# Two inverse roots as a GpSimd power and a log sigmoid from the sigmoid, in a hybrid encoder block

## The chip, the cores and the metric

The kernel runs on one core of a Trainium2 chip. The metric is the device time of one execution in microseconds (us). Before the change the median of three runs is 942.79 us (942.76 to 943.74).

## The reference, cut to what matters

One layer on a sequence of 512 tokens with 1024 features, all in float32: a half-step feed-forward, a mixer of two branches, a second half-step feed-forward and a last norm. The two places that the change touches are in the mixer:

```python
def layer_norm(x, g, b):
    mu = jnp.mean(xf, axis=-1, keepdims=True)
    xc = xf - mu
    y = xc * lax.rsqrt(jnp.mean(xc * xc, axis=-1, keepdims=True) + EPS)
    return (y * g + b)
...
u = a * jax.nn.sigmoid(g)                       # branch A: 512 channels
y = depthwise_causal_conv(u, width=31) + conv_b
y_conv = jax.nn.silu(layer_norm(y, ln_g, ln_b))
...
log_f = jax.nn.log_sigmoid(f_logit)             # branch B: 8 heads of 64
cum = jnp.cumsum(log_f, axis=1)
s = q @ k.T * scale + cum[q] - cum[k]           # causal softmax, times v
...
y = concat([rms_norm(y_conv, out_norm_conv), rms_norm(y_attn, out_norm_attn)])
x = x + y @ w_out
```

The convolution branch thus has two norms in a row: the layer norm over its channels and, after the swish, the RMS norm of the branch output. Each needs 1/sqrt(mean square + 1e-6) for every token.

## The kernel before, in words

Features lie on the 128 partitions and the 512 tokens along the free dimension. TensorE multiplies in a reduced float32 form; each weight and each activation is held as a high and a low part, and a product is three matmuls per block of 128 (high by high, low by high, high by low). Every weight tile of 128x1024 is loaded on SyncE's queue, rounded by ScalarE into `whi` and subtracted by VectorE into `wlo` (`cast`, lines 507 to 510). This goes on through the whole kernel, three loads ahead and two splits ahead.

The program is written as a list of operations for a planner (class `Plan`, lines 172 to 388). `record` takes each operation and its dependences, `price` (lines 252 to 293) gives it a planned duration, and `schedule` (lines 295 to 382) simulates the engines and sets the order of the instructions on each of them: at each step the operation that can start earliest, ties broken by a rank that is the planned length of what hangs on it plus an urgency. ScalarE's functions that need an activation table name it, a change of table is planned at 1.3 us (`SWITCH`, line 175) and lowers the rank by 40 (`PENALTY`, line 81). On the chip each engine then runs its list strictly in order and waits only for semaphores. A changed price, operation or engine thus may change the order everywhere behind it. The loads of the activation tables themselves are not in the program; they are put in ahead of a function that the active table lacks.

The mixer's pieces are listed in `ORDER` (line 60): `c0 c1 c2 v c3 a0 a1 n a2 a3 w0 w1 w2 w3`. Here `c` is the projection, gate (a sigmoid on ScalarE) and convolution of one tile of 128 channels; the 31 taps of tiles 1 and 3 run on VectorE, those of tiles 0 and 2 as a scaled copy on ScalarE and an addition on GpSimd. `v` (`values`, lines 963 to 1020) is the projection of the values and the forget gates, `a` is the attention of two heads (lines 1047 to 1157), `n` the norms of the convolution branch (`conv_norm`, lines 1160 to 1180) and `w` the output projection.

The log sigmoid (lines 1003 to 1016) is computed on a 128x32 tile: ScalarE gives p = exp(-|z|), and VectorE then computes min(z, 0) - 2 artanh(p / (p + 2)) with a series, sixteen instructions joined into one block.

A norm's statistic goes through the class `Stats`: squares, a sum over the partitions by matmuls into a compact 128x128 tile of PSUM (`ssq_*`, 4 groups of 32 partitions for 4 groups of 128 tokens), then `rstd` (lines 594 to 607): ScalarE takes the root with scale 1/n and bias eps into `rc_*`, VectorE the reciprocal in place, `spread` lets TensorE copy the result to all partitions (`rb_*`), and ScalarE copies that to SBUF (`rstd_*`). `conv_norm` calls this twice, for `ln` and for `conv`. Its squares are GpSimd's (`sq_ln`, `sq_conv`), the subtraction of the mean and the multiplication by the scale VectorE's (`acc`), the swish and the high part `yh` ScalarE's, and the low part `yl` VectorE's. All other norms of the kernel call `rstd` in the same way.

In the traces nearly every instruction has line 248, where the planner emits it; instructions are told apart by their tiles.

Of the kernel before, what the change touches and what calls it, by code (L numbers as in the profile page):

```python
# [32 lines left out]
AF = mybir.ActivationFunctionType  # L33
ALU = mybir.AluOpType
AX = mybir.AxisListType

P = 128
# [134 lines left out]
class Plan:  # L172
# [79 lines left out]
    def price(self, op, engine, method, args, kwargs, out):  # L252

        n = out.n if isinstance(out, View) else 512
        if engine == "PE":
            if method != "matmul":
                return n * 0.00084, None
            part = args[1].at[0].size / P
            if args[1].buf.dt != F32:
                return 0.0133 + n / 2400.0, None  # L260
            if part > 0.5:
                return 2 * max(0.02 + n * 0.00069, 0.1), None
            op.tiled = part
            return (0.13 if part > 0.3 else 0.084) * max(n, 64) / P, None
        if method == "dma_start" and engine != "Q":
            return 0.1, None
        psum = any(isinstance(v, View) and v.buf.psum for v in list(args) + list(kwargs.values()))
        if engine == "S":
            cost = (0.143 if psum else 0.2) + n * 0.00083
            if method == "copy":  # L270
                return cost, None
            if isinstance(kwargs.get("scale"), View) or isinstance(kwargs.get("bias"), View):
                cost += 0.09
            if "accum_out" in kwargs:
                op.late = 0.1
            return cost, None if args[2] in (AF.Copy, AF.Square, AF.Identity) else args[2]
        if engine == "G":
            op.port = 1.0
            return 0.1 + n * (0.00233 if method.startswith("tensor_") else 0.0008), None
        if engine == "Q":  # L280
            op.bytes += n * 4 * P
            return 0.4, None
        if method == "tensor_tensor_scan":
            return 0.06 + n * 0.0022, None
        if method == "reciprocal":
            return 0.15 + n * 0.0062, None
        if method in ("tensor_copy", "tensor_scalar") and not psum:
            return 0.15 + n * 0.0006, None
        if not psum:
            op.port = 1.0  # L290
        if method == "scalar_tensor_tensor":
            return 0.15 + n * 0.00118, None
        return 0.15 + n * 0.00105, None
# [106 lines left out]
def block_kernel(ctx: ExitStack, tc, x_d, w13a, w2a, wag, wvf, wqk, wo, w13b, w2b, par_d, out_d):  # L400
    nc = tc.nc
    plan = Plan(tc)
    V, S, PE = plan.engine("V", nc.vector), plan.engine("S", nc.scalar), plan.engine("PE", nc.tensor)
    G, Q = plan.engine("G", nc.gpsimd), plan.engine("Q", nc.sync)
# [6 lines left out]
    def tile_(shape, tag, name, bufs=1, dt=F32):  # L411
        return plan.tile(sb, shape, dt, tag, name, bufs)

    def bank(tag, name, bufs=1):
        return plan.tile(pp, [P, T], F32, tag, name, bufs)

    def product_bank(name):
        return bank("mm", name, 3)
# [22 lines left out]
    eps = tile_([P, 1], "eps", "eps")  # L441
    G.memset(eps, EPS)
    scrap = tile_([P, 57], "scrap", "scrap")[:, :1]
    with plan.urgent(6000.0):
# [4 lines left out]
    ident16 = tile_([P, P], "ident16", "ident16", 1, BF16)  # L449
    G.affine_select(out=ident16, in_=ones, pattern=[[-1, P]], compare_op=ALU.is_equal, fill=0.0,  # L450
                    base=0, channel_multiplier=1)
    sel = tile_([P, NT, P], "sel", "sel")
    G.memset(sel, 0.0)
    mask16 = tile_([P, P], "mask16", "mask16", 1, BF16)
# [17 lines left out]
    for w13, w2 in ((w13a, w2a), (w13b, w2b)):  # L472
# [6 lines left out]
        if w13 is w13a:  # L479
            for piece in ORDER.split():  # L480
                n = int(piece[1:] or 0)
# [52 lines left out]
    class Stats:  # L534
# [56 lines left out]
            plan.join(None)  # L591
            return pb

        def rstd(self, keep=True):
            if self.acc is not None:
                self.sum([self.acc] + self.wait, True)
            w = self.w
            with plan.urgent(URGENT_STATS):
                c = self.compact = tile_([P, P], "rc", f"rc_{self.name}", 2)[:, :w]
                S.activation(c, self.ps[:, :w], AF.Sqrt, bias=eps, scale=1.0 / self.n)  # L600
                V.reciprocal(c, c)
                pb = self.spread(c)
                if not keep:
                    return pb
                r = tile_([P, T], "rstd", f"rstd_{self.name}", 2)
                S.copy(r, pb)
            return r
# [3 lines left out]
    def in_turn(step):  # L611

        for o in stream:
            step.before[id(o)] = o
# [282 lines left out]
    w = tile_([P, 2, KD, P], "vt", f"w{EARLY}", 1, F32R)  # L897
# [65 lines left out]
    def values():  # L963
        plan.urgency = URGENT_V
        pr = bank("misc", "pr", MISC)
        PE.transpose(pr[:, :P], st.compact, ident)
        rcol = tile_([P, NT], "rcol", "rcol")
        V.tensor_copy(rcol, pr[:, 0:P:32])
        plan.urgency = 0.0
        for c in range(2):  # L970
            pv = [product_bank(f"pv{c}_{t}") if t < 2 else bank("s", f"pv{c}_{t}", 2) for t in range(NT)]
            for kh in range(2):
                hi, lo = unit()
                for t in range(NT):
                    ts_ = slice(t * P, (t + 1) * P)
                    o = pv[t][:, :VC]
                    head = None
                    for k in range(KD // 2):
                        kk = kh * (KD // 2) + k
                        step = plan.join("PE", head)  # L980
                        if head is None:
                            head = step
                            in_turn(step)
                        PE.matmul(o, xh[kk][:, ts_], hi[:, k], start=kk == 0, stop=False)
                        PE.matmul(o, xh[kk][:, ts_], lo[:, k], start=False, stop=False)
                        PE.matmul(o, xl[kk][:, ts_], hi[:, k], start=False, stop=kk == KD - 1)
                        plan.join(None)
                    stream[:] = [step]
            plan.urgency = URGENT_V
            for t in range(NT):  # L990
                rc = rcol[:, t:t + 1]
                S.activation(vt[:, t, 4 * HD * c:4 * HD * (c + 1)], pv[t][:, :4 * HD], AF.Copy, scale=rc)
                V.scalar_tensor_tensor(zf[:, t, 4 * c:4 * c + 4], pv[t][:, 4 * HD:VC], rc,
                                       par[:, G_FB + 4 * c:G_FB + 4 * c + 4], ALU.mult, ALU.add)
            plan.urgency = 0.0

        plan.urgency = URGENT_LF
        lf, e1, e2, e3 = (tile_([P, NT, H], n, n) for n in ("lf", "e1", "e2", "e3"))  # L1000
        ps = plan.tile(pp, [P, 16, NT, H], F32, "pt", "e", PT)
        p1, p2, p3, p4 = (ps[:, n] for n in range(4))
        V.scalar_tensor_tensor(e1, zf, -1.0, zf, ALU.mult, ALU.min)
        S.activation(p1, e1, AF.Exp)
        plan.join("V")
        V.tensor_scalar(p2, p1, 2.0, None, ALU.add)
        V.reciprocal(e2, p2)
        V.tensor_mul(p3, p1, e2)
        V.tensor_mul(e1, p1, e2)
        V.tensor_mul(p4, p3, e1)  # L1010
        V.tensor_scalar(e3, p4, 1.0 / 17.0, None, ALU.mult)
        for n in (15, 13, 11, 9, 7, 5, 3):
            V.scalar_tensor_tensor(e3, e3, 1.0 / n, p4, ALU.add, ALU.mult)
        V.scalar_tensor_tensor(e3, e3, 1.0, p3, ALU.add, ALU.mult)
        V.tensor_scalar(p2, zf, 0.0, None, ALU.min)
        V.scalar_tensor_tensor(lf, e3, -2.0, p2, ALU.mult, ALU.add)
        plan.join(None)

        plan.urgency = 0.0
        return lf  # L1020
# [139 lines left out]
    def conv_norm():  # L1160
        ln = Stats("mean", DC)
        for i in range(NC):
            ln.pair(conv[i], i == NC - 1, mean)
        c = tile_([P, P], "rc", "rc_mean", 2)
        S.copy(c, ln.ps[:, :P])
        pm = ln.spread(c)
        ln = Stats("ln", DC)
        for i in range(NC):
            V.tensor_sub(conv[i], conv[i], pm)
            ln.pair(ln.square(conv[i], G), i == NC - 1)  # L1170
        lr = ln.rstd()
        stats = Stats("conv", DC)
        for i in range(NC):
            V.tensor_mul(conv[i], conv[i], lr)
            S.activation(conv[i], conv[i], AF.Silu, bias=par[:, G_LNB + i:G_LNB + i + 1],
                         scale=par[:, G_LNG + i:G_LNG + i + 1])
            stats.pair(stats.square(conv[i], G), i == NC - 1)
            yh[i], yl[i] = slot(2 * i, f"yh{i}", F32R), slot(2 * i + 1, f"yl{i}", F32R)
            split(yh[i], yl[i], conv[i], par[:, G_OC + i:G_OC + i + 1])
        return stats.rstd()  # L1180

    def w_out(part, d, w, r):

# [13 lines left out]
    for piece in ORDER.split():  # L1197
        n = int(piece[1:] or 0)
# [10 lines left out]
        else:  # L1209
# [3 lines left out]
            for j in range(2):  # L1213
                w = unit()
# [59 lines left out]
```

## Time and profile before

| | before |
|---|---|
| median of three runs | 942.79 us |
| the profiled execution's own time | 943.71 us |
| its span in the trace | 942.0 us |
| feed-forward 1 | 0 to about 362 us |
| mixer | about 362 to 577 us |
| feed-forward 2 and the last norm | about 577 to 942 us |
| activation table loads on ScalarE | 15, 1283 ns each |
| GpSimd additions and products of 128x512 | 1292 to 1516 ns by group, 1126 ns for `sq_ln` |

The profile's times are from the start of the span. "PE" is TensorE with its matmuls, "PEld" its weight loads, "DVE" VectorE, "ACT" ScalarE, "POOL" GpSimd and "SP" SyncE, whose queue carries the loads. A row of instructions in time has the start, the duration, the engine, the line, the operation, the output tile and the inputs, the shapes, how many were merged, and in brackets the idle time of the engine before it with what ended it. Matmuls are pipelined and their ends are modelled, so TensorE's busy time says that it had work, not that it ran at its peak.

### The profile page before, as it was taken

What the parts mean: (1) busy time and instruction counts of PE and PEld (TensorE: products, weight loads), DVE (VectorE), ACT (ScalarE), POOL (GpSimd) and SP (SyncE); (2) the same over time, 40 slices, a digit from 0 to 9 for tenths busy, and PEclk for the clock granted to TensorE, in tenths of its full rate; (3) what the DMA queues carried; (4) which work ended last, traced back from release to release, by engine and by line L of the source; (5) the groups of instructions that cost most, each with busy time, mean ns of one, the idle gap of its engine ahead of it and who ended that gap; (6) DMA issues with size and microseconds to landing.
All of it is one profiled execution on the core that took longest, in us unless ns stands there. A gap on an engine that the chain in (4) does not pass through costs nothing.

```text
span 942.0 us, 13470 instructions
## 1 busy us (share of the span) xinstructions
PE 930.2 (99%) x5277; PEld 794.3 (84%) x5277; DVE 655.2 (70%) x990; ACT 434.2 (46%) x678; POOL 154.7 (16%) x132
## 2 busy tenths in 40 slices
PE   9999999999999999999999999999999999999997
PEld 7888999988999888897776777888899988999887
DVE  6655877756876475799987776555777755876554
ACT  7433433334333245676878655333433333433344
POOL 1000211001112000889763000000111001111000
PEclk9999999999999999999999999999999999999999
DMA  7222323132333133323211222222332222323122
GB/s 253 85 92 93 131 90 112 69 107 73 134 112 107 51 97 104 91 93 110 91 68 47 66 67 90 90 90 95 125 117 90 90 90 90 124 100 98 65 84 90
DMA packets 34207, 91.19 MB, mean 97 GB/s; under 512 B 3544, under 2 KB 13912, under 8 KB 34144
## 3 DMA queue, kind: packets, MB, share of 16 engines
q1 hardware_dynamic: 33600, 90.13, 29.0%
q8 instruction: 41, 0.67, 0.3%
q10 hardware_dynamic: 544, 0.20, 0.1%
q14 instruction: 22, 0.18, 0.1%
HBM read 88.21 MB, written 2.11 MB: 96 GB/s over the span
## 4 chain that ended last, share of the span: by engine, by line
PE 92%; DVE 4%; ACT 2%; issue 1%; DMA 1%; SPq 0%; DVEq 0%
PE f2g L248 13%; PE f2u L248 13%; PE f1u L248 13%; PE f1g L248 13%; PE f1p L248 9%; PE f2p L248 9%; PE wo L248 5%; PE f1o L248 3%; PE f2o L248 3%; PE s L248 2%; PE pg L248 2%; PE pa L248 2%; DVE conv L248 2%; PE pq L248 1%; PE pk L248 1%; PE po L248 1%
## 5 line engine op out<-in xcount | busy, mean ns | idle before, releaser
L248 ACT CAST whi<-raw 128x1024 fp32r<-128x1024 f32 (+3 forms) x152 | 150.9, 993 | 263.9 <-issue 84.5
L248 DVE TENSOR_TENSOR wlo<-raw,whi 128x1024 fp32r<-128x1024 f32 (+3 forms) x152 | 185.1, 1219 | 17.8 <-ACT whi L248 17.8
L248 POOL TENSOR_TENSOR acc<-acc,tap 128x512 f32<-128x512 f32 x60 | 90.9, 1516 | 83.5 <-ACT tap L248 79.9
L248 PE MATMUL f1u<-xh,whi 128*128 128x512 f32 x176 | 68.8, 391 | 0.6 <-ACT xh L248 0.6
L248 PE MATMUL f1u<-xl,whi 128*128 128x512 f32 x176 | 68.6, 390 | 0.3 <-DVE xl L248 0.3
L248 PE MATMUL f2g<-xh,whi 128*128 128x512 f32 x176 | 68.7, 390 | 0.0
L248 PE MATMUL f2g<-xl,whi 128*128 128x512 f32 x176 | 68.6, 390 | 0.0
L248 PE MATMUL f2u<-xh,whi 128*128 128x512 f32 x176 | 68.6, 390 | 0.0
L248 PE MATMUL f1u<-xh,wlo 128*128 128x512 f32 x176 | 68.5, 389 | 0.0
L248 PE MATMUL f2u<-xl,whi 128*128 128x512 f32 x176 | 68.5, 389 | 0.0
L248 PE MATMUL f2u<-xh,wlo 128*128 128x512 f32 x176 | 68.5, 389 | 0.0
L248 PE MATMUL f2g<-xh,wlo 128*128 128x512 f32 x176 | 68.5, 389 | 0.0
L248 PE MATMUL f1g<-xh,whi 128*128 128x512 f32 x168 | 65.8, 392 | 0.0
L248 PE MATMUL f1g<-xl,whi 128*128 128x512 f32 x168 | 65.7, 391 | 0.0
L248 PE MATMUL f1g<-xh,wlo 128*128 128x512 f32 x168 | 65.4, 389 | 0.0
L248 POOL TENSOR_TENSOR f2S<-raw 128x512 f32<-128x512 f32 x8 | 11.1, 1384 | 311.8 <-DMA raw<-w2b 295.4
L248 DVE TENSOR_TENSOR f2un<-f2u,rstd_f2in 128x512 f32<-128x512 f32 x22 | 15.2, 691 | 63.6 <-PE f2u L248 63.6
L248 POOL TENSOR_TENSOR f1S<-raw 128x512 f32<-128x512 f32 x8 | 10.3, 1292 | 261.9 <-DMA raw<-w2a 243.7
L248 DVE TENSOR_TENSOR f1un<-f1u,rstd_in 128x512 f32<-128x512 f32 x22 | 15.2, 690 | 54.1 <-PE f1u L248 54.1
L248 ACT ACTIVATE tap<-u,par 128x512 f32<-128x512 f32 x60 | 42.4, 720 | 15.2 <-POOL acc L248 15.0
L248 DVE SCALAR_TENSOR_TENSOR conv<-u,par,conv 128x512 f32<-128x512 f32 x60 | 45.1, 752 | 1.1
L248 PEld LDWEIGHTS f1u<-xh,whi 128*128 128x128 f32 x176 | 33.1, 188 | 8.0 <-ACT xh L248 1.1
(420 smaller groups left out, 2412.7 us busy)
## 6 DMA issues: line engine op xcount, KB each, us to landing
raw<-w13b SPq DMA_DIRECT2D x44, 512.0 KB, 3.5
raw<-w13a SPq DMA_DIRECT2D x42, 512.0 KB, 3.5
raw<-w2a SPq DMA_DIRECT2D x16, 512.0 KB, 3.6
raw<-w2b SPq DMA_DIRECT2D x16, 512.0 KB, 3.5
raw<-wag SPq DMA_DIRECT2D x8, 512.0 KB, 3.5
raw<-wqk SPq DMA_DIRECT2D x8, 512.0 KB, 3.5
raw<-wo SPq DMA_DIRECT2D x8, 512.0 KB, 3.5
raw<-w2a SPq DMA_DIRECT2D x16, 192.0 KB, 2.4
```

The source lines that it names most:

```text
L248: ins = getattr(target, method)(*real, **kw)
```

## The change

In `conv_norm` both norms call `rstd(root=False)`. ScalarE then writes mean square + eps (an Identity with the same scale and bias) and GpSimd raises it to the power of -1/2, element by element, against a 128x128 tile that is filled with -0.5 at the start. The planner is given a price for the power. All other norms keep root and reciprocal. In the log sigmoid ScalarE gives p = sigmoid(-|z|) in place of exp(-|z|), and the first VectorE instruction forms 2 - p in place of p + 2, since exp(-|z|) / (exp(-|z|) + 2) = p / (2 - p).

```diff
@@ price
         if engine == "G":
             op.port = 1.0
+            if ALU.pow in args:
+                return 0.1 + n * 0.02, None
             return 0.1 + n * (0.00233 if method.startswith("tensor_") else 0.0008), None
@@ block_kernel
+    minus = tile_([P, P], "minus", "minus")
+    G.memset(minus, -0.5)
@@ Stats
-        def rstd(self, keep=True):
+        def rstd(self, keep=True, root=True):
...
-                S.activation(c, self.ps[:, :w], AF.Sqrt, bias=eps, scale=1.0 / self.n)
-                V.reciprocal(c, c)
+                if root:
+                    S.activation(c, self.ps[:, :w], AF.Sqrt, bias=eps, scale=1.0 / self.n)
+                    V.reciprocal(c, c)
+                else:
+                    S.activation(c, self.ps[:, :w], AF.Identity, bias=eps, scale=1.0 / self.n)
+                    G.tensor_tensor(c, c, minus, ALU.pow)
                 pb = self.spread(c)
@@ values
-        S.activation(p1, e1, AF.Exp)
+        S.activation(p1, e1, AF.Sigmoid)
         plan.join("V")
-        V.tensor_scalar(p2, p1, 2.0, None, ALU.add)
+        V.tensor_scalar(p2, p1, -1.0, 2.0, ALU.mult, ALU.add)
         V.reciprocal(e2, p2)
@@ conv_norm
-        lr = ln.rstd()
+        lr = ln.rstd(root=False)
...
-        return stats.rstd()
+        return stats.rstd(root=False)
```

## The prediction

> **What bounds the kernel now.** I read the page's engine shares and clock first, then the table of stages, then TensorE's own waits, because an engine that is busy nearly all the time can gain only where it waits.
>
> ```profile
> span 942.0 us, 13470 instructions
> PE 930.2 (99%) x5277; PEld 794.3 (84%) x5277; DVE 655.2 (70%) x990; ACT 434.2 (46%) x678; POOL 154.7 (16%) x132
> ```
>
> ```profile
> core 0: us, PE busy (x) PEld busy (x) DVE busy (x) ACT busy (x) POOL busy (x), PEclk, DMA share, GB/s
> 405.00:447.00 42.00, 40.22 (x240) 35.33 (x238) 40.38 (x68) 29.85 (x43) 37.55 (x25) 1.00 0.32 102
> ...
> 499.00:514.00 15.00, 13.50 (x103) 10.00 (x103) 9.66 (x18) 14.91 (x26) 4.55 (x4) 1.00 0.20 71
> 514.00:530.00 16.00, 16.00 (x131) 12.58 (x130) 13.67 (x26) 12.80 (x27) 3.74 (x5) 1.00 0.10 34
> ```
>
> The columns are the stretch, its length, and the busy time of TensorE (PE), its weight loads, VectorE (DVE), ScalarE (ACT) and GpSimd (POOL), then the granted clock, 1.00 in every stretch. TensorE is busy all of 514 to 530 us; it falls short by 1.78 us in 405 to 447 (VectorE busy 40.38 of 42) and by 1.50 us in 499 to 514, where ScalarE is busy 14.91 of 15. The next view, TensorE's waits from 360 to 580 us (what waited, releaser, us in total, times, longest), gives the same two and one of 0.4 us.
>
> ```profile
> PE s L248 <- DVE k L248: 1.8, 1, 1.8
> PE pt L248 <- ACT pT L248: 1.5, 1, 1.5
> PE s L248 <- DVE mn L248: 0.4, 1, 0.4
> ```
>
> So 3.7 us is all that any relief of the other engines can return in the mixer, and only the middle 1.5 us stands behind ScalarE. This is what I price the change against.
>
> **The change part by part: the norms.** ScalarE's list around the two norms (start, us, instruction), then VectorE's:
>
> ```profile
> 499.95 1.28 ACT L248 ACT_TABLE_LOAD   x1
> 501.25 0.37 ACT L248 ACTIVATE rc_ln<-ssq_ln,eps 128x128 f32<-128x128 f32 x1
> 501.89 1.28 ACT L248 ACT_TABLE_LOAD   x1
> 504.93 0.56 ACT L248 COPY rstd_ln<-rb_ln 128x512 f32<-128x512 f32 x1
> 505.39 1.05 ACT L248 CAST whi<-raw 128x1024 fp32r<-128x1024 f32 x1
> 506.46 1.28 ACT L248 ACT_TABLE_LOAD   x1
> 507.75 1.52 ACT L248 ACTIVATE acc<-acc,par 128x512 f32<-128x512 f32 x2
> 513.04 0.46 ACT L248 COPY pT<-pt 128x384 f32<-128x384 f32 x1
> 520.10 1.28 ACT L248 ACT_TABLE_LOAD   x1
> 521.40 0.37 ACT L248 ACTIVATE rc_conv<-ssq_conv,eps 128x128 f32<-128x128 f32 x1
> 525.51 1.28 ACT L248 ACT_TABLE_LOAD   x1
> ```
>
> ```profile
> 502.02 0.95 DVE L248 RECIPROCAL rc_ln<-rc_ln 128x128 f32<-128x128 f32 x1
> 511.25 0.88 DVE L248 SCALAR_TENSOR_TENSOR yl<-acc,par,yh 128x512 fp32r<-128x512 f32 x1 [0.57 <-ACT yh L248]
> 521.80 0.95 DVE L248 RECIPROCAL rc_conv<-rc_conv 128x128 f32<-128x128 f32 x1 [1.14 <-ACT rc_conv L248]
> ```
>
> Before, the tables go exponential, root (499.95), exponential (501.89), swish (506.46), root (520.10), exponential (525.51). With an Identity in place of the root, which the planner counts as needing no table, the sequence is exponential, swish, exponential: three of the five loads go, 3 x 1.28 = 3.84 us of ScalarE, of which 2.56 us stand ahead of the 1.5 us wait. The Identity has the root's shape and operands, so 0.37 us. Two reciprocals leave VectorE, 2 x 0.95 = 1.90 us, in stretches where it is busy 9.66 of 15 and 13.67 of 16 us: no term.
>
> GpSimd gains two powers of 128x128, which the trace does not show. The nearest rows:
>
> ```profile
> L248 POOL TENSOR_TENSOR f1S<-raw 128x512 f32<-128x512 f32 x8 | 10.3, 1292 | 261.9 <-DMA raw<-w2a 243.7 <-DVE x L248 18.3
> L248 DVE TENSOR_TENSOR acc<-acc,rstd_ln 128x512 f32<-128x512 f32 x4 | 2.5, 688 | 0.3 <-ACT rstd_ln L248 0.3
> ...
> 96.66 1.29 POOL L248 TENSOR_TENSOR f1S<-raw 128x512 f32<-128x512 f32 x1 [93.17 <-DMA raw<-w2a]
> ```
>
> Low end: as cheap per element as that add, 1292/4 = 0.32 us. High end: VectorE's reciprocal costs 950 ns on 128 columns against 688/4 = 172 ns for its product, 5.5 times; the same factor on GpSimd is 1.8 us for one such function, and a power taken as three of them (logarithm, product, exponential) is 5.3 us, an estimate. Between them I take the planner's own price in the diff, 0.1 + 128 x 0.02 = 2.66 us, because its other prices meet their rows: 0.1 + 512 x 0.00233 = 1.29 us for the 1292 ns add, 0.15 + 128 x 0.0062 = 0.94 us for the 0.95 us reciprocal.
>
> Now the chain of the first norm. Its sum and its spread on TensorE, and GpSimd's list there:
>
> ```profile
> 499.06 0.64 PE L248 MATMUL ssq_ln<-sq_ln,ones 128*32 128x128 f32 x16
> 503.39 1.05 PE L248 MATMUL rb_ln<-rc_ln,sel 128*128 128x128 f32 x8
> ...
> 508.70 2.88 POOL L248 TENSOR_TENSOR sq_conv<-acc 128x512 f32<-128x512 f32 x2 [10.62 <-ACT acc L248]
> 519.51 1.63 POOL L248 CAST k<-k 64x512 fp32r<-64x512 f32 x2 [3.28 <-ACT k L248]
> ```
>
> The sum is there by 499.70. Identity 499.95 to 500.32, power to 503.0 (GpSimd is idle for the 10.62 us before 508.70, so nothing queues behind it), spread 503.05 to 504.1 against 503.39 to 504.44 before: this link is 0.3 us earlier. The larger part comes behind it: ScalarE, 2.56 us less loaded, can copy the scale at 504.1 to 504.7. The swish load follows to 506.0, so the first swish starts 1.75 us earlier than 507.75; if the 1.05 us weight cast still lies between, 0.7 us earlier. I take the middle, 1.2 us. TensorE's wait:
>
> ```profile
> 513.55 0.55 PE L248 MATMUL pt<-ident,sm 128*128 128x128 f32 x3 [1.50 <-ACT pT L248]
> ```
>
> TensorE works without a wait up to 512.05 and then stands for the copy of 513.04, which is queued behind the swishes; the next step of the output product waits for the yl of 511.25 (done 512.13) as well. Both hang on the swish chain and come 1.2 us earlier, so 1.2 of the 1.50 us goes. Ends of this term: -1.5 (all of the wait) and 0.
>
> The second norm: Identity 520.10 to 520.47; GpSimd is at the copies of k until 521.14; the power then ends at 523.1 to 523.8, where the spread stood before:
>
> ```profile
> L248 PE MATMUL rb_conv<-rc_conv,sel x8: 270/275/275, 523.8 to 524.6; 128*128 128x128 f32 x8
> ```
>
> Term 0, hidden by TensorE's products of wo and s, which kept it busy 16.00 of 16 us. If the planner sets the power ahead of the two copies, they and the scores that read them come up to 2.66 us later; without that cover the cost is 2.66 us. One thing more could cost: a VectorE operation on two SBUF operands stretches beside GpSimd.
>
> ```profile
> 512.85 2.81 POOL L248 TENSOR_TENSOR sq_conv<-acc 128x512 f32<-128x512 f32 x2
> ...
> 514.68 2.06 DVE L248 TENSOR_TENSOR wlo<-raw,whi 128x1024 fp32r<-128x1024 f32 x1
> ```
>
> GpSimd's products ended at 515.66, and the wlo begun at 514.68 ended 1.08 us after that, as if it had waited for them. The windows of the powers, 500.3 to 503.0 and 521.1 to 523.8, hold on VectorE mainly reciprocals and operations that read PSUM, so I book 0; one wlo or k caught there would be up to 2.66 us late, in front of a TensorE that has other products to do.
>
> **The gates.** ScalarE and VectorE around the log sigmoid, and TensorE's wait behind it:
>
> ```profile
> 421.89 1.28 ACT L248 ACT_TABLE_LOAD   x1
> 423.19 0.20 ACT L248 ACTIVATE e<-e 128x32 f32<-128x32 f32 x1
> 427.62 1.28 ACT L248 ACT_TABLE_LOAD   x1
> ...
> 422.56 0.75 DVE L248 SCALAR_TENSOR_TENSOR conv<-u,par,conv 128x512 f32<-128x512 f32 x1
> 423.42 0.20 DVE L248 TENSOR_SCALAR e<-e 128x32 f32<-128x32 f32 x1
> ...
> 444.95 0.46 PE L248 MATMUL s<-k,q 128*128 128x128 f32 x2 [1.78 <-DVE k L248]
> ```
>
> With a sigmoid of -|z| the gates use the table that the convolution's own gate already has: two loads go, 2.56 us of ScalarE. The VectorE instructions stay sixteen, one of them with a constant more. VectorE waited only 423.42 - 423.31 = 0.11 us for ScalarE here, and the next wait of TensorE, 18 us later, is for VectorE. So the term is 0: the cover is VectorE's 40.38 busy of 42 us. Its ends are the whole 1.8 + 0.4 us if the new order puts the k of 444.95 sooner, and +0.75 us, one more convolution step ahead of it.
>
> The extra constant is one small memset on GpSimd at the start, some 500 us before anything reads it: 0. No DMA is added or moved to another queue; those that follow the mixer come earlier by what TensorE gains.
>
> **The sum.** -1.2 (first norm) + 0 (second) + 0 (gates) = -1.2 us: the profiled execution's 943.71 us would be 942.5, its span 940.8. That execution lies 0.92 us above the median of 942.79, so the median becomes 941.6; I write 941.5.
>
> **The rivals.** (1) The order of VectorE improves too. Every price that changed reorders the planner's list, and VectorE's k is late by about two 0.75 us convolution steps; GpSimd's taps also wait less for ScalarE once the two loads go. For it: the wait is one instruction's place in a list. Against: VectorE's total there does not fall. Time: 941.5 - 2.2 = 939.3.
>
> (2) Nothing comes out: the weight cast and the copies stay where they were, the swish chain starts as late as before, and the 1.5 us remains: 942.8.
>
> (3) Slower: the power is longer than planned. TensorE's order is fixed, so the spreads wait in line. It decides from 503.39 - 500.32 = 3.1 us on at the first norm and from about 3 us at the second, each microsecond above being paid twice. At the high end of 5.3 us that is 2.2 + 2.2 = 4.4 us, less what ScalarE still returns (up to 1.2): 942.8 + 3.2 = 946.0. Against: the planner's prices meet the rows. For: no row shows a power.
>
> (4) Slower: the first power pays for loading its code. In this trace GpSimd's first add, at 96.66 us, took 1.29 us like the mean of its group, so nothing of the kind shows for the operations that are there. TensorE's cover at the first norm is the 0.3 us above, and with a start-up above 1.5 us the gain is gone. For its size I take the high end of a power once more, 5.3 us, an estimate: 5.3 - 0.3 = 5.0 us of wait, 942.8 + 5.0 - 1.2 = 946.6. The Trainium skill (GPSIMD Engine Reference, section 2.1 on instruction dispatch) says that the first call to a freshly loaded kernel pays about 6 us with no visible instruction; by that figure it would be an estimated 947.3. The 1.29 us of the first add does not show it, and no run so far can for a power.
>
> (5) The change may not do what it says: if an Identity or a Sigmoid brought loads of its own, 15 loads would stay; the time is then that of (2).
>
> **How the numbers follow.** About 0.2%, 1.9 us, is what a measurement of this kernel can tell from no change: faster means below 940.9, slower above 944.7. Forecast 0.45 (its own range 940.4 to 942.5, a third of it below 940.9), rival 1 0.23, rivals 2 and 5 0.13, rival 3 0.14, rival 4 0.05. Faster: 0.23 + 0.15 = 0.38. Slower: 0.14 + 0.05 = 0.19. Same: the rest, 0.43. The range goes from 938.8, just past rival 1, to 945.6, short of the worst of 3 and 4; some 0.08 lies below and 0.11 above.
>
> **What would show each step.** 10 table loads in place of 15, none at the two roots, would show that part right; a power near 2.7 us, ending by 503.1, its price; a wait of TensorE before pt under 0.5 us near 512, the gain; an unchanged wait for k near 445, the zero of the gates. A power above 3.1 us with TensorE waiting at rb_ln or rb_conv would make the prediction wrong on the slow side; a wait for k that is gone, on the fast side.

## The result and the profile after

The changed kernel takes 983.66 us (median of five, 983.64 to 984.89) against 942.79 us before (median of five by then, 942.53 to 944.92); the ratio is 1.0428, 95% interval 1.0416 to 1.0439. It is 40.9 us slower, where 941.5 us was forecast. The page of the profile, its engine shares and the clock line of its 40 slices:

```profile
span 982.1 us, 13473 instructions
PE 935.3 (95%) x5277; PEld 797.5 (81%) x5277; DVE 655.4 (67%) x988; ACT 427.8 (44%) x673; POOL 195.9 (20%) x135
...
PEclk9999999999999999999987699999999999999999
```

VectorE has the busy time of before, ScalarE 6.4 us less, and GpSimd 41.2 us more. That this is close to the 40.9 us that the kernel lost is chance: some 7 us of the powers are hidden behind other work, and other losses, told below, make up for them. Two instructions carry it (groups on GpSimd of the changed kernel, mean ns of one after the busy time):

```profile
L248 POOL TENSOR_TENSOR rc_ln<-rc_ln,minus 128x128 f32<-128x128 f32 x1 | 21.6, 21579 | 3.1 <-PE s L248 3.1
L248 POOL TENSOR_TENSOR rc_conv<-rc_conv,minus 128x128 f32<-128x128 f32 x1 | 21.1, 21112 | 0.1
```

A power of 128x128 takes 21.6 and 21.1 us, eight times the planned 2.66. TensorE's waits from 360 to 640 us, as they answer to the three of before:

```profile
PE rb_ln L248 <- POOL rc_ln L248: 18.6, 1, 18.6
PE rb_conv L248 <- POOL rc_conv L248: 16.7, 1, 16.7
PE s L248 <- DVE k L248: 1.5, 1, 1.5
PE po L248 <- ACT pT L248: 0.9, 1, 0.9
PE s L248 <- DVE mn L248: 0.5, 1, 0.5
PE pt L248 <- ACT pT L248: 0.2, 1, 0.2
```

35.3 us of waiting at the two spreads is new; the old waits went from 3.7 to 3.1 us. The stages around the two powers (columns as in the table of stages before):

```profile
core 0: us, PE busy (x) PEld busy (x) DVE busy (x) ACT busy (x) POOL busy (x), PEclk, DMA share, GB/s
...
504.00:522.50 18.50, 0.00 (x0) 0.00 (x0) 0.00 (x0) 0.32 (x1) 18.46 (x1) 0.59 0.03 11
522.50:528.00 5.50, 5.49 (x27) 4.09 (x28) 2.69 (x5) 3.32 (x7) 0.00 (x0) 0.53 0.00 0
528.00:534.00 6.00, 5.76 (x43) 4.16 (x42) 5.78 (x8) 5.98 (x10) 3.99 (x4) 1.00 0.25 87
...
560.60:566.00 5.40, 5.28 (x21) 4.67 (x22) 1.56 (x4) 2.54 (x5) 0.67 (x2) 0.57 0.00 0
```

In these 18.5 us of the power TensorE and VectorE stand, and ScalarE works for 0.32 us. And for about 5 us after each wait TensorE has work again but is granted only part of its clock, 0.53 and 0.57 as the mean of the two rows; by these rows that is 5.5 x 0.47 + 5.4 x 0.43 = 4.9 us of lost clock on top of the waits. In finer slices of the same trace the granted clock falls to 0.50 some 3.3 and 4.2 us after TensorE has stopped, and is back at 1.00 some 5.2 and 4.5 us after it has begun again. The Trainium skill (TensorE: Matmul & The Clock Gate, part 1 on the clock gate) says that the clock is halved after an idle window of about 3.4 us and returns after about as much sustained work. The trace agrees on the half and nearly on the fall; the return took 1 to 2 us longer here.

### The profile page after: what moved, and what is told of

The parts are those of the page before. It is cut to its first block, busy times and chain, and to the rows that moved or that the text cites. A ratio compares the mean times of both kernels' runs of the same rounds, so it can differ in the third digit from the quotient of the medians.

```text
span 982.1 us, 13473 instructions
## 1 busy us (share of the span) xinstructions
PE 935.3 (95%) x5277; PEld 797.5 (81%) x5277; DVE 655.4 (67%) x988; ACT 427.8 (44%) x673; POOL 195.9 (20%) x135
```

## The experiments

Theory: the duration of the power is the loss; TensorE's fixed order makes it a wait, and the clock adds to it. Rivals: the gates or the new order carry part of it; the power's cost is a start-up; the two norms are a chain that no order can cover. Every ratio is against the kernel before, timed beside it on the same chip.

**The gates alone.** Both norms call `rstd()` as before; the sigmoid stays.

> Both norms keep root and reciprocal; the log sigmoid alone comes from the sigmoid. If the whole loss sits in the two powers (theory), this lies within 1.5 us of the kernel before, 941.3 to 944.3 us, with 13 table loads and TensorE's wait for k near 445 us still 1 to 2 us. If the new order of the planner or the gates carry part of the loss (rival), it is 945 us or more.

943.45 us, ratio 0.9992 (0.9983 to 1.0000), 13 table loads, and TensorE's waits in the mixer nearly as before:

```profile
PE s L248 <- DVE k L248: 1.5, 1, 1.5
PE pt L248 <- ACT pT L248: 1.5, 1, 1.5
PE s L248 <- DVE mn L248: 0.4, 1, 0.4
```

The gates cost nothing and give nothing that this measurement can tell.

**A multiplication in the power's place, same order.** The order of the instructions is that of the changed kernel on every engine.

```diff
-            if ALU.pow in args:
+            if ALU.mult in args and n == P:
                 return 0.1 + n * 0.02, None
...
-                    G.tensor_tensor(c, c, minus, ALU.pow)
+                    G.tensor_tensor(c, c, minus, ALU.mult)
```

> The changed kernel with the same order on every engine, but GpSimd's two powers are replaced by a multiplication with the same constant tile, so the two norms are left uncomputed (their scale is wrong). It tells what the rest of the change does when the step on GpSimd is short. My sum of the prediction says 941.5 us (940.4 to 942.5), no wait of TensorE at the two spreads, the wait before 514 us under 0.5 us. If the loss came from the order and not from the power's duration (rival), most of the 41 us stays, over 965 us. The granted clock should be back at 0.998 if its dip comes from TensorE's waiting.

945.20 us, ratio 1.0008 (0.9999 to 1.0017), clock 0.997. The two products took 1.23 and 0.80 us, and the waits at the spreads are gone; the wait before 514 us, expected under 0.5 us, is 1.0 us, with 0.5 us more for GpSimd's squares. So 1.0428 - 1.0008 = 4.20%, 39.6 us, is the power's duration and what follows from it. But the gain of 1.2 us that the prediction had booked did not come either. ScalarE's list of this run:

```profile
499.33 1.05 ACT L248 CAST whi<-raw 128x1024 fp32r<-128x1024 f32 x1 [0.20 <-PE pq L248]
500.29 0.36 ACT L248 ACTIVATE rc_ln<-ssq_ln,eps 128x128 f32<-128x128 f32 x1
...
504.69 0.58 ACT L248 COPY rstd_ln<-rb_ln 128x512 f32<-128x512 f32 x1 [0.52 <-PE rb_ln L248]
505.30 0.62 ACT L248 ACTIVATE sm<-sm,mn 128x384 f32<-128x384 f32 x1
...
506.63 1.28 ACT L248 ACT_TABLE_LOAD   x1
507.93 1.53 ACT L248 ACTIVATE acc<-acc,par 128x512 f32<-128x512 f32 x2
```

The planner moved a weight cast ahead of the Identity and put two exponentials between the scale's copy and the swish load (the first is the row of 505.30). The first swish starts at 507.93, where it started at 507.75 before: what two loads freed went into other work.

**The power on 4 columns.** Each of the 512 values stands 32 times in the 128x128 tile. Here TensorE transposes the tile, VectorE picks 4 columns, GpSimd takes the power of 128x4, and TensorE spreads them by products with the identity. The planner's price of a power is set to 0.1 + 0.165 n us for n columns.

```diff
-                return 0.1 + n * 0.02, None
+                return 0.1 + n * 0.165, None
...
-                    G.tensor_tensor(c, c, minus, ALU.pow)
...
+                    PE.transpose(pr[:, :P], c, ident)
...
+                    V.tensor_copy(q, pr[:, 0:P:32])
+                    G.tensor_tensor(q, q, minus[:, :NT], ALU.pow)
...
+                    for g in range(NT):
+                        PE.matmul(pb[:, g * P:(g + 1) * P], q[:, g:g + 1].columns(P), ident, start=True, stop=True)
...
```

> The 128x128 statistic holds each of 512 values 32 times over; here TensorE transposes it, VectorE picks 4 columns, and GpSimd takes the power of 128x4; the spread goes by a product with the identity. If the power costs 165 ns per column (theory), it takes 0.7 to 0.9 us and the kernel is at 940.5 to 943.5 us. If a power has a large fixed cost whatever its size (rival), it takes over 10 us and the kernel is above 960 us.

942.99 us, ratio 0.9989 (0.9980 to 0.9998): the loss is gone, and it is the best kernel of the study, by 0.1%.

```profile
L248 POOL TENSOR_TENSOR rq_conv<-rq_conv,minus 128x4 f32<-128x4 f32 x1 | 1.4, 1442 | 1.3 <-DVE rq_conv L248 1.3
L248 POOL TENSOR_TENSOR rq_ln<-rq_ln,minus 128x4 f32<-128x4 f32 x1 | 1.0, 1034 | 2.8 <-DVE rq_ln L248 2.8
```

The power took 1.0 and 1.4 us, above the 0.7 to 0.9 expected, but what is left beside the columns' share is only about 0.4 to 0.8 us, so a large fixed cost is ruled out.

**The cost of a power by itself.** The kernel before, with five powers that nothing reads, in GpSimd's idle time of the first 97 us.

```diff
...
+    S.activation(varied, xs[0][:, :P], AF.Square)
+    G.tensor_tensor(probe[:, :32], varied[:, :32], minus[:, :32], ALU.pow)
+    G.tensor_tensor(probe[:, :64], varied[:, :64], minus[:, :64], ALU.pow)
+    G.tensor_tensor(probe, varied, minus, ALU.pow)
+    G.tensor_tensor(probe[:1], varied[:1], minus[:1], ALU.pow)
+    G.tensor_tensor(probe, ones, minus, ALU.pow)
```

> The kernel before, with five powers of -1/2 that nothing reads, put on GpSimd while it is idle in the first 97 us: 128x32, 128x64 and 128x128 of squared inputs, 1x128 of them, and 128x128 of ones. If the cost is per column and the same for any number of partitions and any value (theory), they take 5.4, 10.6, 21.2, 21.2 and 21.2 us. If it is per element of a core's 16 partitions (rival), 1x128 takes about 1.4 us. If values matter (rival), the ones differ from the squares. If the first power pays for loading its code (rival), the first is about 6 us above a line through the next two. VectorE's operations on two SBUF operands beside it show whether the power holds the port: about 1.2 us per 128x1024 subtraction if not, over 5 us if so.

Its groups on GpSimd, and one of VectorE's subtractions beside the powers, which ran from 6.89 to 87.32 us:

```profile
L248 POOL TENSOR_TENSOR probe<-ones,minus 128x128 f32<-128x128 f32 x1 | 21.8, 21761 | 0.1
L248 POOL TENSOR_TENSOR probe<-varied,minus 1x128 f32<-1x128 f32 x1 | 21.4, 21422 | 0.1
L248 POOL TENSOR_TENSOR probe<-varied,minus 128x128 f32<-128x128 f32 x1 | 20.8, 20795 | 0.1
L248 POOL TENSOR_TENSOR probe<-varied,minus 128x64 f32<-128x64 f32 x1 | 10.7, 10679 | 0.1
L248 POOL TENSOR_TENSOR probe<-varied,minus 128x32 f32<-128x32 f32 x1 | 5.5, 5455 | 3.2 <-ACT varied L248 3.2
```

```profile
32.32 1.22 DVE L248 TENSOR_TENSOR wlo<-raw,whi 128x1024 fp32r<-128x1024 f32 x1
```

From 32 to 64 columns 5.22 us, from 64 to 128 10.12 us: 163 and 158 ns per column. One partition costs what 128 cost, and ones cost what varied values cost, both within 5% (20.8 to 21.8 us). The first power is the smallest and lies on the line (5.46 us against 5.22 for 32 columns more); it also began only 0.15 us after the square that it waited for, so no start-up of rival 4's kind stands in it or in front of it. The Trainium skill (GPSIMD Engine Reference, section 2.1) has about 6 us for a first call to freshly loaded code, without a visible instruction. This run shows no such time, and GpSimd's idle time before the power was 3.24 us in all. The subtractions with two SBUF operands took 1.22 to 1.23 us, as without a power: it does not hold VectorE up. The kernel's single time was 944.07 us beside 944.01.

**The planner told 21.2 us.** The price alone is changed.

```diff
             if ALU.pow in args:
-                return 0.1 + n * 0.02, None
+                return 0.1 + n * 0.165, None
```

> The changed kernel with the planner's price of the power set to the measured one, 0.1 + 128 x 0.165 = 21.2 us, and nothing else. If most of the loss is TensorE standing in a fixed order in front of a result that the planner thought ready (theory), the planner puts other products ahead of the two spreads: waits at the spreads together under 15 us instead of 35.3, and 945 to 962 us. If the two powers lie on a chain that nothing can cover (rival), the waits only move to another instruction and the time stays above 972 us.

980.43 us, ratio 1.0385 (1.0370 to 1.0401): the theory's range was missed and the time is the rival's. The waits at the spreads fell only to 16.0 and 10.4 us:

```profile
PE rb_ln L248 <- POOL rc_ln L248: 16.0, 1, 16.0
PE rb_conv L248 <- POOL rc_conv L248: 10.4, 1, 10.4
```

One reason could be read in this run: the plan books any GpSimd operation as holding a port that VectorE's two-operand operations need, so it saw VectorE blocked for 21 us. The rows (GpSimd, then VectorE) show a subtraction at its usual duration in the middle of the power:

```profile
497.28 21.51 POOL L248 TENSOR_TENSOR rc_ln<-rc_ln,minus 128x128 f32<-128x128 f32 x1 [0.98 <-ACT rc_ln L248]
...
503.75 1.23 DVE L248 TENSOR_TENSOR wlo<-raw,whi 128x1024 fp32r<-128x1024 f32 x1 [3.59 <-ACT whi L248]
```

**The same, with the port free in the plan.**

```diff
-            op.port = 1.0
             if ALU.pow in args:
                 return 0.1 + n * 0.165, None
+            op.port = 1.0
```

> As the run in which the planner was told 21.2 us, but the power is also planned as not holding the port that GpSimd and VectorE share, because VectorE's operations on two SBUF operands ran beside the power at their usual 1.23 and 0.69 us. If the wrong port in the plan was what kept other products out of the wait (theory), the scores and products of heads 4 to 7 move ahead of the first spread: its wait falls from 16.0 us to under 8, and the kernel to 950 to 970 us. If the two norms are a chain that the order cannot cover (rival), it stays within 3 us of 980.4.

976.82 us, ratio 1.0340 (1.0325 to 1.0356): slower than the theory's range, 3.6 us faster than the run before, and with a new picture:

```profile
PE rb_conv L248 <- POOL rc_conv L248: 18.8, 1, 18.8
PE wo L248 <- ACT yh L248: 4.7, 1, 4.7
...
PE rb_ln L248 <- POOL rc_ln L248: 0.8, 1, 0.8
```

```profile
535.01 21.49 POOL L248 TENSOR_TENSOR rc_conv<-rc_conv,minus 128x128 f32<-128x128 f32 x1 [2.33 <-ACT rc_conv L248]
556.45 0.52 POOL L248 MEMSET k<- 64x512 f32 x1
```

The first wait is gone, as the theory had it: the port in the plan had caused it. The second grew. The second fence, GpSimd's list, names a suspect: the zeroing of half a k tile, which the scores of the last heads need, stands behind the second power.

**Nothing behind the power that the scores need.** On top of the last edit:

```diff
-                G.memset(f32(l)[other], 0.0)
+                V.memset(f32(l)[other], 0.0)
...
-                G.tensor_copy(h[other], h[own])
+                S.copy(h[other], h[own])
```

> As the run with the planner told and the port free, and in addition the zeroing of k's low half is VectorE's and the copy of its high half ScalarE's in the last two attention pieces, so that nothing that the scores need stands in GpSimd's list behind a power. If the second wait of 18.8 us came from those instructions queueing behind the second power (theory), the scores of the last heads run during it: TensorE's wait at the second spread falls below 12 us and the kernel to 958 to 970 us. If the products of the last heads have to wait for the second norm itself, through full PSUM banks or buffers (rival), the wait stays above 16 us and the time at 975 to 978 us.

962.35 us, ratio 1.0191 (1.0174 to 1.0208). The time and the second wait are as the theory expected:

```profile
PE wo L248 <- ACT yh L248: 4.1, 1, 4.1
PE rb_ln L248 <- POOL rc_ln L248: 3.6, 1, 3.6
PE pt L248 <- ACT pT L248: 2.8, 4, 0.7
PE po L248 <- ACT pT L248: 2.6, 5, 1.4
PE rb_conv L248 <- POOL rc_conv L248: 1.7, 1, 1.7
```

The waits at the spreads are 5.3 us in place of 35.3, though the powers still take 20.8 us each. The five waits shown come to 14.8 us, and all waits of the mixer to 12.8 us more than before the change; the granted clock, 0.50 from 524.3 to 530 us and 0.86 in the 3 us after, accounts by these rows for some 3.3 us more of the 18 that are still lost. So more than half of the loss, 1.0428 to 1.0191, was not the power's duration alone but an order, and a placement of small instructions, made without knowing it. The step from 1.0340 to 1.0191 is the largest; its two lines of code took eight instructions off GpSimd's list, and the planner also made a new order around them, so the two are not told apart.

**TensorE kept busy.** The order of every engine is the changed kernel's; 20 products that nothing reads stand in front of each spread.

```diff
+FILL = 20
...
+            if self.name in ("ln", "conv"):
+                for n in range(FILL):
+                    PE.matmul(pb, f32(xl[0])[:, :P], f32(xh[0]), start=True, stop=True)
+                plan.joined.cost = 0.0
```

> The changed kernel with every engine's order the same, and 20 float32 products of 128x512 that nothing reads put in front of each of the two spreads, so that TensorE works while it would stand. If the clock's dip after each wait costs time beyond the wait (theory), the granted clock returns to 0.998 and the kernel is 4 to 6 us faster than the changed one: 978 to 980 us, provided the filling ends before the powers do. If the dip is only seen in idle time and costs nothing (rival), the time stays at 983 to 985 us.

981.21 us, ratio 1.0391 (1.0373 to 1.0409) against 1.0428 (1.0416 to 1.0439): 0.37%, 3.5 us, less (2.7 us by the spans of the two traces), though TensorE does some 35 us more work. Its stages after the first wait and after the second:

```profile
522.50:528.00 5.50, 5.50 (x39) 4.27 (x40) 3.75 (x9) 4.41 (x8) 0.28 (x1) 1.00 0.00 0
...
560.00:566.00 6.00, 6.00 (x39) 5.02 (x38) 3.94 (x12) 3.58 (x10) 0.26 (x1) 1.00 0.00 0
```

The clock is 1.00 where it was 0.53 and 0.57. The dip cost time beyond the wait; the 3.5 us are a little under the 4 to 6 expected, and 981.21 us a little above the 978 to 980. TensorE still stood 1.4 us at the first spread, and the second filling ended 0.5 us after the power that it covered.

**The norms on 4 columns, gates as before; and the same with the right price.** The first takes the sigmoid out again; the second keeps it and changes the plan of the small power, which the run on 4 columns had at 0.1 + 0.165 n.

```diff
-        S.activation(p1, e1, AF.Sigmoid)
+        S.activation(p1, e1, AF.Exp)
...
-        V.tensor_scalar(p2, p1, -1.0, 2.0, ALU.mult, ALU.add)
+        V.tensor_scalar(p2, p1, 2.0, None, ALU.add)
```

```diff
-            op.port = 1.0
             if ALU.pow in args:
-                return 0.1 + n * 0.165, None
+                return 0.4 + n * 0.165, None
+            op.port = 1.0
```

> The power on 4 columns as before, but the gates keep the exponential: 12 table loads in place of 15 (three go in the norms). If the gain of 0.1% of the run on 4 columns comes from the norms (theory), the ratio to the kernel before is 0.998 to 0.9995 and the first swish starts about 2 us earlier than 507.75; if it comes from the gates (rival), it is 0.9995 to 1.001.

> Power on 4 columns and sigmoid gates, with the planner told what the power on 4 columns took, 0.4 + 4 x 0.165 = 1.06 us, and that it does not hold the shared port. If the order is by now near what the engines allow (theory), the ratio stays at 0.998 to 0.9995; if TensorE's wait of 1.0 us for the second norm's transpose was an order made with a wrong price (rival), it goes and the ratio is 0.997 to 0.998.

Ratios 0.9996 (0.9987 to 1.0005) and 1.0000 (0.9991 to 1.0009). The first lies in the rival's range, but its interval reaches into the theory's; the swish starts at 506.25, 1.5 us earlier than before, without a gain that can be told. TensorE's waits in the mixer show one reason:

```profile
PE s L248 <- DVE k L248: 1.8, 1, 1.8
PE tr_conv L248 <- ACT rc_conv L248: 1.0, 1, 1.0
PE s L248 <- DVE mn L248: 0.4, 1, 0.4
```

The 1.5 us wait before 514 us is gone, as it is in the first run on 4 columns, but 1.0 us has come in its place at the second norm's transpose. In the second run here that wait is gone as its rival had it, yet a wait for a pT copy (1.0 us) and one for GpSimd's squares (0.5 us) are there instead, and the ratio is above both expected ranges. This run has the work of the kernel at 0.9989 with better prices and is no faster, so the 0.1% of that kernel is of the size of a change of order, and where it comes from stays open.

**The multiplication, planner told 0.5 us.** The two norms are left uncomputed as before.

```diff
             if ALU.mult in args and n == P:
-                return 0.1 + n * 0.02, None
+                return 0.5, None
```

> As the run with a multiplication in place of the power (the two norms are left uncomputed), but the planner is told 0.5 us for it instead of 2.66, so the order may change. If the 1.2 us of the prediction were lost because an order planned for 2.66 us put ScalarE's casts and exponentials ahead of the scale's copy (theory), the swish load moves ahead of 506.6 us and the ratio falls to 0.998 to 0.9995. If ScalarE's freed time cannot be turned into time at all (rival), it stays at 1.000 to 1.002.

946.24 us, ratio 1.0024 (1.0015 to 1.0033): just above the rival's range, and not by the rival's way. The swish load did move ahead, to 503.63 us, and TensorE waited all the same:

```profile
504.93 1.52 ACT L248 ACTIVATE acc<-acc,par 128x512 f32<-128x512 f32 x2
...
510.58 1.28 ACT L248 ACT_TABLE_LOAD   x1
...
512.60 0.46 ACT L248 COPY pT<-pt 128x384 f32<-128x384 f32 x1
```

```profile
PE pt L248 <- ACT pT L248: 1.4, 1, 1.4
PE po L248 <- ACT pT L248: 0.9, 2, 0.4
```

The swishes start 2.8 us earlier than before the change, but the copy that TensorE waits for starts only 0.4 us earlier (512.60 against 513.04): the order has put the load of the exponential's table and an exponential between the swishes and it. TensorE's waits for pT copies are 1.4 + 0.9 us instead of 1.5. What makes this run 0.2% slower than before beyond these waits was not found.

## Why the prediction was wrong, point by point

**The step that failed** is the price of the power: "Between them I take the planner's own price in the diff, 0.1 + 128 x 0.02 = 2.66 us, because its other prices meet their rows." It measured 21.6 and 21.1 us, and alone in the trace 20.8 us, 162 ns per column. So it was eight times as long as booked, and far above the 3.1 us that the prediction itself had named as the sign of being wrong on the slow side. That the planner's other prices met rows said nothing of one that had no row. The high end, 5.3 us, was no bound: it was built as three times a reciprocal, whose ratio to a product had been measured on VectorE and carried over to GpSimd.

**The mechanism of rival 3 was right and its size off.** It said that TensorE's order is fixed, that it decides from 3.1 us on at the first norm and about 3 us at the second, and that each microsecond above is paid twice. With the measured durations it gives (21.6 - 3.1) + (21.1 - 3.0) = 36.6 us; the waits are 35.3. It left out the clock after the waits, 3.5 us by the run that kept TensorE busy (2.7 by the spans, 4.9 by the clock rows), and the rest of the change with its new order, 0.0008 x 942.8 = 0.8 us by the run with the multiplication, whose interval reaches from about 0 to 1.6. 35.3 + 3.5 + 0.8 = 39.6 of the 40.9 us; the rest is within the intervals of the parts.

**The first norm, -1.2 us**: wrong as well, and hidden by the larger miss. With the power out of the way, the change is at 1.0008 (0.9999 to 1.0017). Two things failed in turn. "ScalarE, 2.56 us less loaded, can copy the scale at 504.1": the planner put casts and exponentials there, and the first swish stayed at 507.93. And "both hang on the swish chain and come 1.2 us earlier, so 1.2 of the 1.50 us goes": this holds only as long as the copy of pT stays right behind the swishes. In the two runs on 4 columns that had the small power at the planner's 0.1 + 0.165 n, it did: the swishes came 1.5 and 2.3 us earlier, the 1.50 us wait was gone, and a new one of 1.0 us came at the second norm's transpose. In the last run the swishes came 2.8 us earlier, but a table load and an exponential stood between them and the copy, and the wait stayed. A wait that an order makes moves with the order.

**Table loads**: 10 in place of 15, as forecast. They were worth nothing that can be told, as the prediction itself had it for three of the five.

**The gates, 0**: right, 0.9992 (0.9983 to 1.0000), with the wait for k near 445 us still 1.5 us.

**The second norm, 0**: wrong by the price. Its condition, "if the planner sets the power ahead of the two copies", came about: one of the two stood at 560.73, behind the power's end. The price given for that, 2.66 us, was the power's again.

**VectorE held up beside a power**: booked at 0, rightly, but for a reason that was not needed. The rows that I showed were of additions and products; a power does not do it, at 1.22 us per subtraction beside it. **Rival 4**, a start-up: not there. **Rival 1**, the wait for k gone: no, 1.8 became 1.5 us. **The chances**: 0.14 lay on the right mechanism, and the range ended at 945.6, since its slow end came from the 5.3 us.

## What to carry to other kernels

An operation that has no row has no price, whatever model quotes one: bound it by what happens if it is ten times as long, or measure it off the path first. On an engine with an in-order list, a long instruction costs what stands behind it as much as what reads it: here two lines of another piece, eight small instructions, moved off GpSimd's list, with the order that the planner then made, returned a third of the loss. And where a value is held many times over, compact it before a costly elementwise step: 4 columns in place of 128 made the power 1.0 to 1.4 us.

## What the runs showed of the hardware

GpSimd's power took 158 to 163 ns for each column more, and 20.8 to 21.8 us for 128 columns whether on 1 partition or on 128, of ones or of varied values. Beside it VectorE's subtraction of two SBUF operands ran at its usual 1.22 us, unlike beside GpSimd's products, where one took 2.06 us. TensorE's granted clock was 0.50 for 5.2 and 4.5 us after waits of 18.6 and 16.7 us, and 1.00 where products that nobody read filled the waits.
